# One attention step split in two, the mLSTM gates moved ahead of the convolution, and a new order of the first loads in a two-layer hybrid trunk

## The chip, the cores and the metric

The kernel runs on one core of one Trainium2 chip. The metric is the device time of one execution in microseconds (us). Before the change three runs gave 2652.69, 2652.71 and 2653.03 us, median 2652.71 us.

## What is computed

A trunk of two layers on 1024 tokens of width 1024. Each layer projects the normalised input once and gives its columns to three groups of heads, called mixers here; then come an output projection, an MLP and a gated extra input, each added to x:

```python
h = rms_norm(x);  y = h @ w_in + b_in
m_out = mlstm(...)      # 4 heads x 64: causal conv + SiLU on q and k, gates, chunkwise state
h_out = hgrn2(...)      # 4 heads, state 64 x 64, chunkwise gated recurrence
s_out = swa(...)        # 8 query heads, 2 kv heads x 64, window 128, one sink per head
x = x + concat(m_out, h_out, s_out) @ w_out
x = x + square(relu(rms_norm(x) @ w_up)) @ w_down
x = x + sigmoid(rms_norm(x) @ w_g) * rms_norm(p[l] @ w_p)
```

In the attention the probabilities are `exp(s - m) / (sum exp(s - m) + exp(sink - m))`. In the mLSTM the gates are cumulative sums and running maxima over time of the two pre-activations `mi` and `mf`; the convolution works on q and k alone, so neither needs the other before the scores are weighted.

## The kernel before, in words

The tokens are cut in two halves b = 0, 1 of 512, and every dense product works on one half. A dense product (`gemm`, lines 409 to 441) keeps fp32 accuracy with three products per weight tile: each operand is split in a high part (`whi`, ACT, line 395) and a low rest (`wlo`, DVE, line 399), and high x high, high x low and low x high are added up in PSUM. One step of `gemm` is one pair of weight tiles: 24 matmuls of 128x512 on TensorE (lines 435 and 437). There are four `whi` and four `wlo` buffers, two steps' worth.

The mixers are Python generators: `SWA` (attention), `HGRN` and `MLSTM`, one for each 256 tokens of a half. Each `yield` ends one mixer step. The `Emitter` runs the dense work as the main program and, after each dense step, adds `rate` to a counter and emits one mixer step for every whole one; up to three mixers take turns. The rate is 1.9 and 2.5 in the two input projections of the first layer (`IN(0,0)` and `IN(0,1)`), 0.7 in those of the second, and `RATE_MLP` = 0.9 in the MLP, whose 66 dense steps of a half carry the mixers of the other half. Before a half's output projection `OUT_T` (line 685) transposes the mixers' results. The emission order is a priority; the order in which each engine's instructions finally stand is fixed when the program is built, and each engine works through its own in that order. So an instruction that waits holds up all that stands behind it on its engine.

The places that the change and the prediction touch:

- `SWA`, lines 887 to 1005: one step makes the scores of a block of 128 queries (L969) and the exponentials (L979). The next step divides each of eight heads by its sum (L989, DVE), transposes the probabilities (L999, TensorE) and copies them out (L1001, ACT). In the step after that `values` (L932) multiplies them with V: for each half of the window two matmuls, one per kv head, that write different halves of the columns.
- `MLSTM`, lines 1178 to 1302: step one is the convolution (ACT L1192, twelve DVE operations L1194); step two the two SiLUs of q and k, the copies into `qbd`, and then the gates: transposes L1209 on TensorE, a log-sigmoid on ACT (L1215, L354 to L356), two scans and some small operations on DVE (L1217 to L1231) into `G`. Step three transposes `G` (L1236). Later steps use the SiLU results (L1262), make the products with the state (L1272, L1277, L1283) and end with `head_out`, whose last instruction is L1035.
- `load_x`, lines 520 to 532, makes the first loads: x of the first half on the queues of SP and ACT (L527), and between them the first two tiles of weights `w_skv` (`early`). ACT then issues the `cols` constants (L184), the positions, and one row of biases (L555).
- `first`, lines 1341 to 1350, interleaves the first normalisation `a` with the first projection `c`. The normalisation ends with the root of the mean square (L483 to L349) and its transposes (L574).

In MLP and PLE, L498 transposes the normalised x, L794 transposes p.

Of the kernel before, what the change touches and what calls it, by code (L numbers as in the profile page):

```python
# [16 lines left out]
AF = mybir.ActivationFunctionType  # L17
ALU = mybir.AluOpType
# [20 lines left out]
RATE_IN00 = 1.9  # L39
RATE_IN01 = 2.5  # L40
RATE_IN = 0.7
RATE_MLP = 0.9
RATE_PLE = 0.9

ROOM = tuple(22 - 4 * max(0, (n + 2) // 4) + 2 for n in range(24)) + (8,)
# [4 lines left out]
C_IN, C_MLP, C_PLE, C_CW, C_CB, C_BF, C_MG, C_LB = 0, 8, 16, 24, 40, 44, 52, 56  # L50
# [106 lines left out]
class Trunk:  # L157
# [362 lines left out]
    def load_x(self, b, src, first=False):  # L520
        X = [[None, None] for _ in range(4)]
        for h in range(2):
            for t in range(4):
                s = X[t][h] = self.get()
                eng = self.nc.gpsimd if not first else self.nc.scalar if (h, t % 2) == (0, 1) else self.nc.sync
                with self.tc.high_priority(2000) if first and h == 0 else nullcontext():
                    end = eng.dma_start(s[:, :512], src(b, t, h))  # L527
                    if first and h == 0 and t == 3:
                        self.x_asked = end
            if first and h == 0:  # L530
                self.early = [self.wraw(self.skv_rows(0, kp)) for kp in range(2)]
        return X

    def x_in(self, b, t, h):
# [352 lines left out]
    def SWA(self, l, b, hb, st):  # L887
        nc, rs = self.nc, self.rs[l]
# [48 lines left out]
        for i in range(2):  # L937
# [25 lines left out]
            for hp in range(4):  # L963
# [8 lines left out]
                for j in range(2):  # L972
                    h = 2 * hp + j
# [3 lines left out]
                for j in range(2):  # L977
                    h = 2 * hp + j
# [8 lines left out]
            for h in range(8):  # L987
                v = PX[h // 2][:, (h % 2) * n:(h % 2) * n + n]
                nc.vector.tensor_scalar(v, v, rsum[:, h:h + 1], None, op0=ALU.mult)  # L989

            vis = (prev, cur)[2 - n // P:]
            pts = [[None, None] for _ in vis]
            for kv in range(2):
                for hf in range(len(vis)):
                    ps = self.bank()
                    for g in range(4):
                        h = kv * 4 + g
                        c = (h % 2) * n + hf * P
# [179 lines left out]
    def MLSTM(self, l, b, hb, st):  # L1178
        nc, cols, ident = self.nc, self.cols[l], self.ident
# [3 lines left out]
        if b == 0 and hb == 0:  # L1183
            nc.gpsimd.memset(self.cbd, 0.0)
            nc.gpsimd.memset(self.ml, 0.0)
        Y = [self.get() for _ in range(2)]
        a = self.get()
        for f in range(4):
            y = Y[f // 2][:, (f % 2) * 256:(f % 2) * 256 + 256]
            u = st["U"][f]  # L1190
            c0 = C_CW + 4 * f
            nc.scalar.activation(y, u[:, hb * 256:hb * 256 + 256], AF.Identity, scale=cols[:, c0:c0 + 1], bias=cols[:, C_CB + f:C_CB + f + 1])  # L1192
            for j in range(1, 4):
                nc.vector.scalar_tensor_tensor(y, u[:, hb * 256 + j:hb * 256 + j + 256], cols[:, c0 + j:c0 + j + 1], y, op0=ALU.mult, op1=ALU.add)  # L1194
        if hb == 1:
            self.put(*st["U"])
        yield
        Q, Kt = Y[0][:, :512], Y[1][:, :512]
        self.silu(Q, a[:, :512])
        self.silu(Kt, a[:, :512], 0.125)  # L1200
        Q3 = Q.rearrange("p (a t) -> p a t", a=2)
        K3 = Kt.rearrange("p (a t) -> p a t", a=2)
        for j in range(2):
            nc.vector.tensor_copy(self.qbd[j * 64:j * 64 + 64, :, j, :], Q3[j * 64:j * 64 + 64])

        pg = self.bank()
        for i in range(2):
# [22 lines left out]
        nc.vector.tensor_copy(Gb[32:36], r1)  # L1230
        nc.vector.tensor_tensor(Gb[64:68], r1, Gb[32:36], op=ALU.subtract)  # L1231
        self.put(g, g2)
        yield
        pt = self.bank()
        for c in range(2):
# [14 lines left out]
        for c in range(2):  # L1250
# [33 lines left out]
            for h in range(4):  # L1284
                r, p = (h % 2) * 64, h // 2
# [13 lines left out]
        self.head_out(H[:, :512], mo[:, :512], a[:, :512], ms, False)  # L1299
        self.put(H, ND, kw, a, *Y, mv)  # L1300
        self.release_kv(st["skv"][hb])
# [3 lines left out]
def chain(*gens):  # L1305
    for g in gens:
        yield from g


@with_exitstack  # L1310
def trunk_kernel(ctx: ExitStack, tc: tile.TileContext, io, dims):
    k = Trunk(ctx, tc, io, dims)
    L = k.L
    assert k.NB == 2
    st = {}
    for l in range(L):
        st[l, 0], st[l, 1] = {}, {}
    em = Emitter(k.S_, WIDTH)
    last = L - 1

    def IN(l, b, between=None):
        return k.IN(l, b, st[l, b], lambda kind: em.queue.extend(k.MIX(l, b, st[l, b], kind)), between)

    def norm(l, b):
        return k.IN_norm(l, b, st[l, b])

    def OUT(l, b):
        if "own" not in st[l, b]:
            em.flush((l, b), 0)
            k.OUT_T(l, b, st[l, b])  # L1330
        em.run(k.OUT(l, b, st[l, b]))

    def tail(l, b, then=None):
        def ready():
            em.flush(then)
            k.OUT_T(*then, st[then])

        em.run(k.MLP(l, b), RATE_MLP)
        em.run(k.PLE(l, b, l == last, ready if then else None), RATE_PLE)

    def first():
        a, c = norm(0, 0), IN(0, 0, norm(0, 1))
        yield next(a)
        yield next(c)
        k.behind = k.last_mm
        yield next(c)
        yield next(a)
        k.behind = None
        yield from a
        yield from c  # L1350

    em.run(first(), RATE_IN00)
    k.bounds()
    em.run(IN(0, 1), RATE_IN01, ROOM, (0, 0))
    OUT(0, 0)
    for l in range(L):
        tail(l, 0, (l, 1))
        OUT(l, 1)
        if l == last:
            tail(l, 1)  # L1360
            break
        em.run(chain(norm(l + 1, 0), IN(l + 1, 0)), RATE_IN)
        tail(l, 1, (l + 1, 0))
        OUT(l + 1, 0)
        em.run(chain(norm(l + 1, 1), IN(l + 1, 1)), RATE_IN)
# [51 lines left out]
```

## Time and profile before

| | |
|---|---|
| median of three runs | 2652.71 us |
| the profiled execution | 2653.13 us |
| its span in the trace | 2651.4 us |
| TensorE busy | 2636.1 us (99%) |
| DVE busy | 1742.0 us (66%) |
| ACT busy | 1401.5 us (53%) |
| granted TensorE clock, mean | 0.999 |

The span is the time from the first to the last instruction in the trace; the execution itself took 1.7 us more. Times in the rows are microseconds from the start of the span. A matmul's end is modelled: matmuls overlap, so the durations of one engine's rows may add up to more than the time between their starts, and a wait is read best from start to start. L12 is line 12 of the kernel before.

### The profile page before, as it was taken

Reading aid. Unit: us, or ns where it says so; the run is one execution under the profiler, and the core shown is the slowest. Engines: PE = TensorE matmul, PEld = TensorE weight load, DVE = VectorE, ACT = ScalarE, POOL = GpSimd, SP = SyncE. Lnnn points to the kernel's source line nnn. Section 1 sums busy time; section 2 is a strip of 40 time slices with the busy share of each in tenths; the row PEclk is TensorE's granted clock in tenths of the full one; section 3 lists DMA queues with packets and bytes.
Section 4 is the critical chain, followed back from the end, with each engine's and each line's share of the span. In section 5 each row is a group of like instructions: output and inputs, shape, how many; then the busy total and the mean of one; then the engine's idle time right before and its main releaser. Section 6 shows DMA issues by size and latency. Waiting matters only on the chain.

```text
span 2651.4 us, 35073 instructions
## 1 busy us (share of the span) xinstructions
PE 2636.1 (99%) x12719; PEld 2143.3 (81%) x12719; DVE 1742.0 (66%) x3697; ACT 1401.5 (53%) x2924; POOL 106.1 (4%) x232
## 2 busy tenths in 40 slices
PE   9999999999999999999999999999999999999999
PEld 7877788887788888887788888888778888888887
DVE  5787757677678557776775755776677584443448
ACT  5456545455557544545654653554664464433336
POOL 3201100000000100000000010000000000000000
PEclk9999999999999999999999999999999999999999
DMA  7644532222222532222222253222222243332332
GB/s 220 199 115 121 144 110 80 88 80 80 84 84 90 151 100 80 88 87 73 80 88 96 97 155 93 77 88 80 78 82 88 96 135 104 96 96 95 104 104 80
DMA packets 138845, 270.54 MB, mean 102 GB/s; under 512 B 10672, under 2 KB 15920, under 8 KB 138672
## 3 DMA queue, kind: packets, MB, share of 16 engines
q1 hardware_dynamic: 119328, 224.03, 27.2%
q0 software_dynamic: 18480, 43.55, 5.5%
q8 instruction: 100, 1.64, 0.3%
q10 hardware_dynamic: 864, 0.72, 0.1%
q14 instruction: 73, 0.60, 0.1%
HBM read 249.39 MB, written 18.87 MB: 101 GB/s over the span
## 4 chain that ended last, share of the span: by engine, by line
PE 95%; DVE 2%; ACT 1%; issue 1%; DMA 1%; POOL 0%; POOLq 0%; ACTq 0%; DVEq 0%
PE gbank L437 52%; PE gbank L435 32%; PE mbank L498 1%; PE mbank L932 1%; PE mbank L999 1%; PE mbank L1142 1%; PE mbank L969 1%; PE gbank L467 1%; PE mbank L1262 1%; PE mbank L1269 1%; PE mbank L1158 0%; PE mbank L1127 0%; PE mbank L945 0%; PE mbank L1272 0%; ACT junk L476 0%
## 5 line engine op out<-in xcount | busy, mean ns | idle before, releaser
L437 PE MATMUL gbank<-whi,slot 128*128 128x512 f32 (+1 forms) x4160 | 1303.2, 391 | 0.0
L395 ACT ACTIVATE whi<-raw 128x512 fp32r<-128x512 f32 (+1 forms) x836 | 515.2, 621 | 830.7 <-PE gbank L437 492.1
L437 PEld LDWEIGHTS gbank<-whi,slot 128*128 128x128 f32 x4160 | 772.1, 188 | 170.4 <-issue 2.8
L399 DVE TENSOR_TENSOR wlo<-raw,whi 128x512 fp32r<-128x512 f32 (+1 forms) x800 | 538.3, 679 | 545.2 <-ACT whi L395 542.2
L435 PE MATMUL gbank<-slot,whi 128*128 128x512 f32 x2560 | 824.7, 397 | 0.0
L437 PE MATMUL gbank<-wlo,slot 128*128 128x512 f32 (+1 forms) x2080 | 807.9, 389 | 0.4 <-DVE wlo L399 0.3
L435 PEld LDWEIGHTS gbank<-slot,whi 128*128 128x128 f32 x2560 | 480.3, 188 | 110.7 <-issue 3.3
L435 PE MATMUL gbank<-slot,wlo 128*128 128x512 f32 x1280 | 505.9, 395 | 0.5 <-DMA wlo<-lo 0.4
L437 PEld LDWEIGHTS gbank<-wlo,slot 128*128 128x128 f32 x2080 | 391.5, 188 | 81.2 <-DVE wlo L399 0.8
L435 PEld LDWEIGHTS gbank<-slot,wlo 128*128 128x128 f32 x1280 | 241.1, 188 | 52.3 <-DMA wlo<-lo 1.3
L759 DVE SCALAR_TENSOR_TENSOR slot<-gbank,nrs,slot 128x512 f32<-128x512 f32 x256 | 191.4, 748 | 48.7 <-PE gbank L437 45.6
L367 DVE TENSOR_TENSOR slot<-slot 128x512 fp32r<-128x512 f32 x144 | 99.1, 690 | 86.9 <-ACT slot L366 86.1
L370 DVE SCALAR_TENSOR_TENSOR slot<-mbank,cols,slot 128x512 fp32r<-128x512 f32 x112 | 78.8, 744 | 20.3 <-ACT slot L369 20.0
L745 ACT ACTIVATE slot<-gbank 128x512 f32<-128x512 f32 x128 | 74.9, 585 | 32.4 <-PE gbank L435 32.3
L366 ACT ACTIVATE slot<-slot 128x512 fp32r<-128x512 f32 x144 | 89.6, 629 | 2.6
L369 ACT ACTIVATE slot<-mbank,cols 128x512 fp32r<-128x512 f32 x112 | 72.3, 686 | 20.7 <-PE mbank L498 14.8
L746 ACT ACTIVATE slot<-slot 128x512 f32<-128x512 f32 x128 | 80.6, 629 | 2.5
L476 ACT ACTIVATE junk<-slot 128x512 bf16<-128x512 f32 x96 | 60.1, 626 | 34.3 <-DVE slot L759 16.9
L979 ACT ACTIVATE slot<-slot,snm 128x256 f32<-128x256 f32 (+1 forms) x128 | 61.8, 484 | 29.2 <-DVE snm L976 29.2
L788 POOL DMA_DIRECT2D slot<-in_p_dram x8 | 5.7, 719 | 1412.1 <-PE gbank L437 469.8
L498 PE MATMUL mbank<-ident,slot 128*128 128x128 f32 x384 | 60.7, 273 | 0.5 <-ACT slot L1259 0.5
L1096 ACT ACTIVATE slot<-slot 128x256 f32<-128x256 f32 x56 | 23.5, 420 | 71.3 <-DVE slot L1095 71.1
(274 smaller groups left out, 2287.3 us busy)
## 6 DMA issues: line engine op xcount, KB each, us to landing
raw<-in_w_up_dram SPq DMA_DIRECT2D x128, 512.0 KB, 3.6
raw<-in_w_down_dram SPq DMA_DIRECT2D x128, 512.0 KB, 3.5
raw<-in_w_in_dram SPq DMA_DIRECT2D x80, 512.0 KB, 3.8
raw<-in_w_ple_gate_dram SPq DMA_DIRECT2D x32, 512.0 KB, 3.5
lo<-wlo POOLq DMA_DIRECT2D x40, 256.0 KB, 4.3
wlo<-lo POOLq DMA_DIRECT2D x40, 256.0 KB, 3.0
raw<-in_w_out_dram SPq DMA_DIRECT2D x16, 512.0 KB, 4.4
raw<-in_w_out_dram SPq DMA_DIRECT2D x32, 256.0 KB, 4.3
```

The lines of the kernel that those rows point to most:

```text
L366: first = nc.scalar.activation(r_(hi), src, AF.Copy)
L367: nc.vector.tensor_tensor(r_(lo), src, hi, op=ALU.subtract)
L369: first = nc.scalar.activation(r_(hi), src, AF.Copy, scale=scale)
L370: nc.vector.scalar_tensor_tensor(r_(lo), src, scale, hi, op0=ALU.mult, op1=ALU.subtract)
L395: nc.scalar.activation(hi[:, :n], raw[:, kk, :n], AF.Copy)
L399: nc.vector.tensor_tensor(lo[:, :n], raw[:, kk, :n], hi.bitcast(F32)[:, :n], op=ALU.subtract)
L435: nc.tensor.matmul(banks[i], wa[:, sl], ta, start=first, stop=last)
L437: self.last_mm = nc.tensor.matmul(banks[i][:, :n], ta, wa[:, :n], start=first, stop=last)
L498: nc.tensor.transpose(ps[:, t * P:(t + 1) * P], X[t][h][:, k4 * P:(k4 + 1) * P], self.ident)
L745: nc.scalar.activation(u[:, :512], ps, AF.Relu)
L746: nc.scalar.activation(u[:, :512], u[:, :512], AF.Square)
L759: nc.vector.scalar_tensor_tensor(x, ps, r2[:, i:i + 1], x, op0=ALU.mult, op1=ALU.add)
```

## The change

Four pieces. The numerical work is the same, instruction for instruction; only the order changes.

- In `SWA` a `yield` is put between the division of the probabilities and their transposes, so these are two mixer steps.
- In `MLSTM` the gates come first, as a step of their own; then the convolution, as before a step; then the SiLUs ("scale"), now a step of their own.
- `RATE_MLP` goes from 0.9 to 1.0. For one half the three kinds of mixers had 64 steps to run, counting the last resumption of each; now there are 70, because each attention mixer has two more and each mLSTM one more.
- The first two `w_skv` loads are to stand behind the second x load of SP, and `first` emits one more step of the projection before the normalisation's end.

```diff
-RATE_MLP = 0.9
+RATE_MLP = 1.0
...
                     if first and h == 0 and t == 3:
                         self.x_asked = end
+                    if first and h == 0 and t == 2:
+                        self.x_sp = end
             if first and h == 0:
-                self.early = [self.wraw(self.skv_rows(0, kp)) for kp in range(2)]
+                with self.tc.issue_after(self.x_sp.ins):
+                    self.early = [self.wraw(self.skv_rows(0, kp)) for kp in range(2)]
...
             for h in range(8):
                 v = PX[h // 2][:, (h % 2) * n:(h % 2) * n + n]
                 nc.vector.tensor_scalar(v, v, rsum[:, h:h + 1], None, op0=ALU.mult)
+            yield
...
     def MLSTM(self, l, b, hb, st):
...
-        Y = [self.get() for _ in range(2)]
-        a = self.get()
-        for f in range(4):
...
-        yield
-        Q, Kt = Y[0][:, :512], Y[1][:, :512]
-        self.silu(Q, a[:, :512])
-        self.silu(Kt, a[:, :512], 0.125)
...
-            nc.vector.tensor_copy(self.qbd[j * 64:j * 64 + 64, :, j, :], Q3[j * 64:j * 64 + 64])
         pg = self.bank()
...
         nc.vector.tensor_tensor(Gb[64:68], r1, Gb[32:36], op=ALU.subtract)
         self.put(g, g2)
+        yield
+        Y = [self.get() for _ in range(2)]
+        a = self.get()
+        for f in range(4):
...
+        yield
+        Q, Kt = Y[0][:, :512], Y[1][:, :512]
+        self.silu(Q, a[:, :512])
+        self.silu(Kt, a[:, :512], 0.125)
...
+            nc.vector.tensor_copy(self.qbd[j * 64:j * 64 + 64, :, j, :], Q3[j * 64:j * 64 + 64])
         yield
         pt = self.bank()
...
     def first():
         a, c = norm(0, 0), IN(0, 0, norm(0, 1))
         yield next(a)
         yield next(c)
         k.behind = k.last_mm
         yield next(c)
         yield next(a)
         k.behind = None
+        yield next(c)
         yield from a
         yield from c
```

How the order of the built program moves is shown at three places. The first is SP's queue at the start of the program; L527 are loads of x, L377 loads of weights. Before:

```order
L527 DMA slot<-in_x_dram 128x512
L377 DMA raw<-in_w_skv_dram 128x2x264
L527 DMA slot<-in_x_dram 128x512
L377 DMA raw<-in_w_skv_dram 128x2x264
L527 DMA slot<-in_x_dram 128x512 x4
L377 DMA raw<-in_w_skv_dram 128x2x264 x2
```

Now:

```order
L527 DMA slot<-in_x_dram 128x512 x2
L377 DMA raw<-in_w_skv_dram 128x2x264 x2
L527 DMA slot<-in_x_dram 128x512 x4
L377 DMA raw<-in_w_skv_dram 128x2x264 x2
L377 DMA raw<-in_w_in_dram 128x2x512 x20
```

SP's second x load has moved ahead of the first weight load; nothing else moved in this queue.

The second place is DVE's queue in `IN(0,1)`, at the first mLSTM: L989 is the last attention division before it, L1194 the convolution, L357 of 128x512 and L1019 belong to the SiLU of q, L357 of 4x256 to L1224 are the gates. Before:

```order
L989 TENSOR_SCALAR slot<-slot,srs 128x256 x8
L1194 SCALAR_TENSOR_TENSOR slot<-slot,cols_93 128x256 x12
L357 SCALAR_TENSOR_TENSOR slot<-slot 128x512
L1019 TENSOR_TENSOR slot<-slot 128x512
L357 SCALAR_TENSOR_TENSOR slot<-slot 4x256
L1204 COPY qbd<-slot 64x2x256 x2
L1217 SCALAR_TENSOR_TENSOR slot<-rmask,slot 4x256
L1218 SCALAR_TENSOR_TENSOR slot<-slot,ml,mbank 4x256
L1221 TENSOR_TENSOR G_345<-mbank,slot 4x256
L357 SCALAR_TENSOR_TENSOR slot<-slot 128x512
L1220 TENSOR_TENSOR G_345<-slot 4x256
L1224 TENSOR_SCALAR G_345<-slot 4x256
```

Now (L992 is the old L989, L1202 to L1216 the old L1217 to L1231, L1227 the old L1194):

```order
L992 TENSOR_SCALAR slot<-slot,srs 128x256 x8
L357 SCALAR_TENSOR_TENSOR slot<-slot 4x256
L1202 SCALAR_TENSOR_TENSOR slot<-rmask,slot 4x256
L1203 SCALAR_TENSOR_TENSOR slot<-slot,ml,mbank 4x256
L1206 TENSOR_TENSOR G_379<-mbank,slot 4x256
L1205 TENSOR_TENSOR G_379<-slot 4x256
L1209 TENSOR_SCALAR G_379<-slot 4x256
L1207 TENSOR_SCALAR G_379<-G_379,ml 4x128
L1208 TENSOR_SCALAR G_379<-G_379,slot 4x128
L1210 COPY ml<-slot 4x1
L1213 CAST Gb<-G_379 4x256
L1227 SCALAR_TENSOR_TENSOR slot<-slot,cols_93 128x256
```

The gates stand alone and ahead of the convolution. On TensorE the distance between the transposes that open the gates (old L1209) and those that close them (old L1236) changes with it: in `IN(0,1)` from 45 and 68 dense matmuls to 19 and 26, in the MLPs from 24 to 51 or 52. In `IN(0,1)` the last products of the mLSTM (old L1283) stand 91 dense matmuls ahead of `OUT_T` (old L685) before the change, and 45 now.

The third place is TensorE in the MLP of the first layer's first half, at the last products of attention with V. Before (L932 are those products, L435 and L437 dense matmuls):

```order
L437 MATMUL gbank<-whi,slot 128x512
L932 MATMUL mbank<-slot,V 64x512
L437 MATMUL gbank<-whi,slot 128x512
L437 MATMUL gbank<-wlo,slot 128x512
L437 MATMUL gbank<-whi,slot 128x512 x2
L437 MATMUL gbank<-wlo,slot 128x512
L437 MATMUL gbank<-whi,slot 128x512
L932 MATMUL mbank<-slot,V 64x512 x2
L437 MATMUL gbank<-whi,slot 128x512
```

Now (L935 is the old L932):

```order
L435 MATMUL gbank<-slot,wlo 128x512
L435 MATMUL gbank<-slot,whi 128x512
L935 MATMUL mbank<-slot,V 64x512 x4
L435 MATMUL gbank<-slot,whi 128x512
L435 MATMUL gbank<-slot,wlo 128x512
L435 MATMUL gbank<-slot,whi 128x512 x2
```

The four products, which were cut 1, 2, 1 by six dense matmuls each, stand together now.

## Rows read from the trace of the kernel before

**Rows 1.** The page, engines: busy time, share of the span, instructions.

```profile
PE 2636.1 (99%) x12719; PEld 2143.3 (81%) x12719; DVE 1742.0 (66%) x3697; ACT 1401.5 (53%) x2924; POOL 106.1 (4%) x232
```

**Rows 2.** The page, the chain that ended last: shares of the span by engine.

```profile
PE 95%; DVE 2%; ACT 1%; issue 1%; DMA 1%; POOL 0%; POOLq 0%; ACTq 0%; DVEq 0%
```

**Rows 3.** The chain in order of time, at 562: start, duration, what.

```profile
562.04 22.21 PE gbank L435 x96
```

**Rows 4.** Timeline, start: start, duration, engine, line [idle before, releaser].

```profile
6.99 1.91 PE L498 MATMUL mbank<-ident,slot 128*128 128x128 f32 x16
7.29 0.40 ACTq L555 DMA_DIRECT2D slot<-in_rowB_dram  x1
7.80 0.69 ACT L369 ACTIVATE slot<-mbank,cols 128x512 fp32r<-128x512 f32 x1 [5.71 <-DMA cols<-in_cols_dram]
...
23.52 0.62 PE L574 MATMUL mbank<-ident,nrs 128*128 128x128 f32 x4 [0.41 <-DVE nrs L349]
```

**Rows 5.** Timeline, TensorE: the two transposes of the gates in IN(0,1).

```profile
267.88 0.41 PE L1236 MATMUL mbank<-ident,G 100*128 100x100 f32 x2 [0.91 <-DVE G L1222]
...
299.50 0.28 PE L1236 MATMUL mbank<-ident,G 100*128 100x100 f32 x1 [1.00 <-DVE G L1222]
```

**Rows 6.** Timeline, ACT and DVE: the gates' chain before the first of them.

```profile
258.57 0.45 ACT L1215 ACTIVATE slot<-mbank,fb 4x256 f32<-4x256 f32 x1
...
262.99 0.41 DVE L357 SCALAR_TENSOR_TENSOR slot<-slot 4x256 f32<-4x256 f32 x1
...
264.20 0.68 DVE L1217 TENSOR_TENSOR_SCAN slot<-rmask,slot 4x256 f32<-4x256 bf16 x1
...
267.45 0.28 DVE L1222 TENSOR_SCALAR G<-G,ml 4x128 f32<-4x128 f32 x1
```

**Rows 7.** Timeline, TensorE and DVE: end of the mixers in IN(0,1).

```profile
313.56 0.61 PE L1283 MATMUL mbank<-slot 128*128 128x130 f32 x4
...
323.48 0.69 DVE L1035 TENSOR_TENSOR slot<-slot 128x512 f32<-128x512 f32 x1 [0.62 <-ACT slot L361]
...
335.14 1.91 PE L685 MATMUL mbank<-ident,slot 128*128 128x128 f32 x16
```

**Rows 8.** Timeline, TensorE: end of the first MLP and its PLE.

```profile
793.96 0.41 PE L1236 MATMUL mbank<-ident,G 100*128 100x100 f32 x2 [0.84 <-DVE G L1222]
...
803.18 0.66 PE L498 MATMUL mbank<-ident,slot 128*128 128x128 f32 x4 [0.55 <-ACT slot L1259]
```

**Rows 9.** Timeline, TensorE: from L1277 to L1283 in one mLSTM chunk.

```profile
274.94 0.38 PE L1277 MATMUL mbank<-ident,slot 128*128 128x128 f32 x2
...
276.08 0.61 PE L1283 MATMUL mbank<-slot 128*128 128x130 f32 x4
```

**Rows 10.** Timeline, TensorE: attention transposes in the MLP of (0,1).

```profile
1201.94 0.40 PE L435 MATMUL gbank<-slot,whi 128*128 128x512 f32 x1
...
1203.58 1.50 PE L999 MATMUL mbank<-ident,slot 128*128 128x128 f32 x7 [0.41 <-DVE slot L989]
1204.84 0.48 PE L437 MATMUL gbank<-whi,slot 128*128 128x512 f32 x1
```

**Rows 11.** Timeline, TensorE: first piece of the V products cut in three.

```profile
700.16 1.07 PE L932 MATMUL mbank<-slot,V 128*64 128x512 f32 x2
701.16 0.50 PE L437 MATMUL gbank<-whi,slot 128*128 128x512 f32 x1
```

**Rows 12.** Timeline, TensorE: V products in one piece.

```profile
634.21 1.94 PE L932 MATMUL mbank<-slot,V 128*64 128x512 f32 x8
636.08 0.50 PE L435 MATMUL gbank<-slot,whi 128*128 128x512 f32 x1
```

**Rows 13.** Busy time in stretches: us, PE, PEld, DVE, ACT, POOL (x instructions), clock, DMA.

```profile
255.01:270.20 15.19, 14.28 (x68) 10.89 (x65) 13.22 (x32) 9.93 (x21) 2.12 (x4) 1.00 0.41 123
...
720.00:760.00 40.00, 39.94 (x202) 32.57 (x201) 22.89 (x47) 18.95 (x40) 1.44 (x2) 1.00 0.30 94
2319.00:2363.00 44.00, 44.00 (x192) 35.77 (x191) 19.09 (x28) 16.47 (x29) 0.00 (x0) 1.00 0.30 96
```

More of the change, by code (lines that the diff above doesn't have):

```diff
@@ L1185, in MLSTM @@
             nc.gpsimd.memset(self.ml, 0.0)
-        Y = [self.get() for _ in range(2)]
-        a = self.get()
-        for f in range(4):
[L1189 to L1196, printed above, removed]
-        yield
-        Q, Kt = Y[0][:, :512], Y[1][:, :512]
-        self.silu(Q, a[:, :512])
-        self.silu(Kt, a[:, :512], 0.125)
-        Q3 = Q.rearrange("p (a t) -> p a t", a=2)
-        K3 = Kt.rearrange("p (a t) -> p a t", a=2)
-        for j in range(2):
-            nc.vector.tensor_copy(self.qbd[j * 64:j * 64 + 64, :, j, :], Q3[j * 64:j * 64 + 64])
         pg = self.bank()
@@ L1232, in MLSTM @@
         self.put(g, g2)
+        yield
+        Y = [self.get() for _ in range(2)]
+        a = self.get()
+        for f in range(4):
+            y = Y[f // 2][:, (f % 2) * 256:(f % 2) * 256 + 256]
+            u = st["U"][f]
+            c0 = C_CW + 4 * f
+            nc.scalar.activation(y, u[:, hb * 256:hb * 256 + 256], AF.Identity, scale=cols[:, c0:c0 + 1], bias=cols[:, C_CB + f:C_CB + f + 1])
+            for j in range(1, 4):
+                nc.vector.scalar_tensor_tensor(y, u[:, hb * 256 + j:hb * 256 + j + 256], cols[:, c0 + j:c0 + j + 1], y, op0=ALU.mult, op1=ALU.add)
+        if hb == 1:
+            self.put(*st["U"])
+        yield
+        Q, Kt = Y[0][:, :512], Y[1][:, :512]
+        self.silu(Q, a[:, :512])
+        self.silu(Kt, a[:, :512], 0.125)
+        Q3 = Q.rearrange("p (a t) -> p a t", a=2)
+        K3 = Kt.rearrange("p (a t) -> p a t", a=2)
+        for j in range(2):
+            nc.vector.tensor_copy(self.qbd[j * 64:j * 64 + 64, :, j, :], Q3[j * 64:j * 64 + 64])
         yield
```

## Prediction, made before the changed kernel was run

> **What bounds the kernel now.** I read the page first. TensorE is busy for 2636.1 of 2651.4 us, 99% [rows 1], and 95% of the chain that ended last is TensorE's own work [rows 2]. A busy TensorE need not be a fast one, so the next view is the chain in order of time: there 96 dense matmuls take 22.21 us [rows 3], 0.231 us each, and the clock column beside such stretches reads 1.00, the 2.4 GHz level [rows 13]. The change removes no matmul. What it can win is the time in which TensorE does nothing, and all of that is 2651.4 - 2636.1 = 15.3 us. Part of it, the wait for the first data and the output after the last matmul, no order removes. So I went through TensorE's timeline and looked for waits over 0.25 us. There are few, and each has a name: at the start [rows 4], at the transposes of the gates [rows 5, 8], at attention's transposes [rows 10] and at products that are cut up [rows 11]. The reader is to see in these rows that the sum is one of single microseconds; 0.2%, or 5.3 us, is about what a measurement of this kernel can tell from no change.
>
> At one point a rule speaks otherwise. By rows, headroom is 15.3 us. The Trainium skill (Perfetto Trace Analysis, Identifying the Most-Contended Engine) holds that the busy share of matmuls says little and that the busy share of weight loads should be used for TensorE; that share is 81% here. By it an estimated 500 us would be open, and a better order could win far more than the list below. The pitch of 0.231 us, which is the same wherever a long run of dense matmuls stands, is why I sum by rows.
>
> **Part 1, the start.** The second x load of SP now goes ahead of a weight load. Before, TensorE's first transposes start at 6.99, and ACT's first use of them at 7.80, after ACT has issued the bias row at 7.29 [rows 4]. In the built program that issue waits for the landing of the second weight load before, and for the smaller constants now. At most the 7.80 becomes 6.99 + 4 x 0.11 (four transposes, 16 in 1.91 us less overlap), a gain of 0.4, if x does not come earlier too; at least nothing. I take 0.3. The next step of the projection is emitted ahead of the normalisation's end, so two more matmuls stand before the transposes L574, which wait for 0.41 us now [rows 4]; the ACT work ahead of them is the same. I take 0.4 of the two kinds of wait there. Together -0.7, between 0 and -1.8 (all the waits of 8 to 24 us and the 0.4).
>
> Here too a rule is weighed. Rows show x, weights and constants all issued in the first 8 us and ACT waiting 5.71 us for the last of what it needs [rows 4]. The Trainium skill (DMA: Bandwidth & Descriptors, Issuing engines are not separate DMA queues) says that all queues end in the same 16 engines and interleave, so moving one load ahead only delays another. By it this term would be 0 instead of -0.7, which the bounds contain.
>
> **Part 2, the first layer's input projections.** Up to the first third of `IN(0,1)` TensorE's order is the same, so its waits there stay. Then come the gates. Before, TensorE idles 0.91 and 1.00 us at L1236 for `G` [rows 5]. The chain to `G` is: ACT L1215 at 258.57, then three operations of 4x256; DVE's log-sigmoid, scans and differences until 267.45 + 0.28 [rows 6], 9.2 us, because the SiLUs and the copies lie between. Alone it is about 1.7 us on ACT (four like L1215's 0.45, or a little less), 0.5 for L357, and 3.5 from L1217 to the end of L1222 less the 0.6 of a SiLU between: some 5.2 us. The first transposes now come 19 dense matmuls, 4.4 us, behind the gates' start: a wait of 0.8. At the second, 26 matmuls, 6.0 us: a wait of 0.2 for what DVE still has. So -0.1 and -0.8, -0.9. What is late next is `head_out`: six more steps at the same rate end the mixers later. From L1283 at 313.56 to the end of L1035 at 323.48 + 0.69 it takes 10.6 us [rows 7]; before, 91 matmuls (21 us) cover that, and L685 comes at 335.14. Now 45 do, 10.4 us, and DVE has the evacuations of the last dense product in between. I add 0.5, between 0 and 2.5 (two such evacuations and one weight split more). Together -0.4, between -1.9 and +2.
>
> **Part 3, the MLPs.** In the MLPs the gates' transposes now have 51 matmuls of cover, 11.8 us against 5.2: the 0.84 of [rows 8] goes, with 0.17 more, since a dense matmul's row lasts 0.40 [rows 10] and its pitch 0.231: -1.0. But at that place the built order now puts L1283 straight behind L1277, and from the one to the other take 1.14 us [rows 9], 0.22 of them two transposes: +0.9. The 0.55 behind it [rows 8] I take as overlapped by this one, -0.4. Together -0.5, between -1.7 and +0.9.
>
> The division step: with a step between, L999 finds its operand ready. In the MLP of (0,1) TensorE goes from 1201.94 to 1204.84 through eight transposes [rows 10]; one pitch of 0.231 and 8 x 0.11 would be 1.11: -1.8. The products with V run two at a time when they stand together: eight in 1.87 us [rows 12]. Cut in three, each piece takes 1.00 us [rows 11], and there are three pieces: 3.0 - 1.87 and two changes between kinds of matmul less, -1.3. Smaller waits of this kind in MLPs I leave out. Together -3.1; at least half of it, -1.5, and at most -3.6.
>
> The rate: 70 steps over 66 dense steps instead of 64 at 0.9 need the same stretch. DVE carries them: 19.09 us per eight dense steps without mixers [rows 13], 2.4 per step of 5.55, and 13.22 for a whole convolution, SiLU and gates [rows 13], now over three steps instead of two. I cost this at nothing, since TensorE has been busy for 39.94 of 40 us in a stretch that has the heavier two-step form [rows 13].
>
> **Part 4, what the new order may cost.** The built order also puts steps of HGRN closer behind the transposes at the start of two MLPs, and cuts some transposes of attention in two. Nothing in the trace of before shows them. Below, 0; above, a wait of 1.0 and one of 0.5 (the sizes of [rows 5, 8]) at each of two places, 3.0. I take +0.7, nearer to nothing, because most of the waits over 0.25 lie in `IN(0,1)`.
>
> **Sum.** -0.7 - 0.4 - 0.5 - 3.1 + 0.7 = -4.0 us. The profiled execution took 2653.13 us, 1.7 more than its span and 0.4 more than the median of 2652.71; from the median it comes to **2648.7 us**.
>
> **The rivals.** *All waits go and none comes.* -1.8 - 1.9 - 1.7 - 3.6 = -9.0; with two thirds of it, 2646.7, with all 2643.7. For it: the waits have names and the change aims at each. Against: in `IN(0,1)` the new cover is shorter, not longer. Chance 0.25.
>
> *The waits move.* `head_out`, L1283 and the start of the MLPs take what the gates and the start gave: -0.7 + 2 + 0.9 + 2 - 3.1 - 1.0 (the one of rows 8) = +0.1, with half of these costs 2650.5, with all 2652.8. For it: 45 matmuls against a chain of 10.6 us. Chance 0.22.
>
> *It does not do what it says.* The final order is not the emission order. If the attention transposes end up waiting as before, only parts 1 and 2 remain, 2651.6. Against: the order shown has the V products together. Chance 0.06.
>
> *DVE becomes the bound, and it is slower.* The three mLSTM steps now fall on three dense steps in a row: 13.2 + 3 x 2.4 = 20.4 us of DVE against 3 x 5.55 + 0.8 = 17.5 of TensorE, 2.9 too much. If the weight splits on DVE are queued behind that, TensorE waits for `wlo`. Six such passes lie in MLPs: +17.4, with -4.0 it gives 2666.1. It decides from the point where the buffers of split weights hold less than 2.9 us of work; they hold one step ahead, 5.55. Against it: before, the two-step form is 13.2 + 2.2 x 2.4 = 18.5 against 2.2 x 5.55 = 12.2, 6 us too much, and TensorE idled 0.06 us there [rows 13]. Chance 0.03.
>
> *The rule on weight loads is right, and much is open.* By rows as a mechanism: if the 0.231 us contained a stall that order removes, the stretches with mixers would have a longer pitch than [rows 3]; they do not. A hundredth of the span, 26 us less, would be 2626. Chance 0.02.
>
> **How the numbers follow.** The forecast itself has 0.42 and reaches from 2646.5 to 2650.5. Faster by over 0.2% (below 2647.4) holds the rule, two thirds of the first rival and a quarter of the forecast: 0.02 + 0.17 + 0.11 = 0.30. Slower by over 0.2% (above 2658.0) is DVE's case and a hundredth for the rest: 0.04. Within 0.2%: 0.66. The range of 8 in 10 leaves out the far ends of the first rival and of the second: 2645.5 to 2652.3.
>
> **What would show it.** Right: in the changed trace no idle time before L999 and L1236 in the MLPs, V products in one piece of about 1.9 us; idle before L1236 of 0.8 and 0.2 in `IN(0,1)`; L685 within a microsecond of the 1152nd dense matmul; ACT's first use of the transposes by 7.5. Wrong: TensorE idle before L435 or L437 for `wlo`, more than 2.5 us before L685, or a start later than before.

## The result, and the profile after

The changed kernel takes 2668.56 us (median of three runs, 2667.18 to 2670.51) against 2652.71 before: 15.85 us slower, ratio 1.0061, 95% interval 1.0043 to 1.0079. The forecast was 2648.7 with a range up to 2652.3, and slower by over 0.2% had 0.04. The range did not hold the time.

The page of the changed kernel, engines and then the chain that ended last, which answer to [rows 1, 2]:

```profile
PE 2639.6 (99%) x12719; PEld 2143.7 (80%) x12719; DVE 1736.9 (65%) x3697; ACT 1396.5 (52%) x2924; POOL 106.4 (4%) x232
...
PE 93%; DVE 5%; ACT 1%; issue 1%; DMA 0%; ACTq 0%; DVEq 0%
```

The span is 2666.8 us, so TensorE is idle for 27.2 us where it was 15.3, and busy for 3.5 us more with the same number of instructions. Both have to be explained: 11.9 us of waits, and 3.5 us in which the same matmuls took longer. VectorE (DVE) has no more to do than before (1736.9 against 1742.0), but its share of the chain went from 2% to 5%. The waits view of TensorE says who is waited for (line waited at, releaser: us in total, times, longest):

```profile
PE gbank L437 <- DVE wlo L399: 9.6, 6, 3.1
PE mbank L1241 <- DVE G L1207: 2.1, 2, 1.2
PE gbank L435 <- DVE slot L762: 1.6, 5, 0.6
...
PE gbank L435 <- DVE wlo L399: 1.3, 2, 0.7
```

Before, `wlo` cost L437 0.3 us in one wait. Now the low halves of the weights (L399) and the evacuations of the down projection (L762) come late. Where? The table gives, for the dense matmul that has the given number of dense matmuls ahead of it, its start in each trace minus its start in the trace of before. A stage's cost is the difference of two rows. The runs e1 to e13 are those of the next section. In the middle of a stage the numbers mean little, because mixers may run earlier or later there; these are ends of stages.

| dense matmul, place | after | e1 | e2 | e3 | e7 | e8 | e9 | e13 |
|---|---|---|---|---|---|---|---|---|
| 1152, end of `IN(0,1)` | 0.3 | 1.2 | 1.1 | -0.9 | 0.3 | -0.3 | 2.8 | 1.5 |
| 3888, start of the MLP (0,1) | 0.0 | 5.2 | 1.7 | -3.5 | -2.4 | -4.0 | 3.7 | 6.3 |
| 5424, its end | 7.2 | 7.6 | 5.3 | -3.3 | -1.8 | -5.9 | 5.0 | 9.0 |
| 6432, start of the MLP (1,0) | 7.7 | 8.7 | 5.9 | -3.2 | -1.3 | -5.6 | 5.3 | 9.4 |
| 7968, its end | 15.0 | 9.8 | 10.0 | -2.3 | 0.4 | -6.3 | 7.9 | 12.0 |
| last | 15.4 | 11.0 | 10.7 | -1.6 | 0.9 | -5.4 | 8.5 | 12.3 |

Nearly all of the net loss is made in two MLPs, 7.2 and 7.3 us. Here is the worst place in the first of them, TensorE's timeline (start, duration, engine, line; in brackets the idle time before it and who ended it):

```profile
1326.81 0.50 PE L437 MATMUL gbank<-whi,slot 128*128 128x512 f32 x1
1327.15 0.34 PE L1260 MATMUL mbank<-Gb,selb 128*128 128x128 bf16 x3
1330.57 0.79 PE L437 MATMUL gbank<-wlo,slot 128*128 128x512 f32 x1 [3.08 <-DVE wlo L399]
...
1332.02 0.63 PE L437 MATMUL gbank<-wlo,slot 128*128 128x512 f32 x1
1332.44 0.63 PE L437 MATMUL gbank<-whi,slot 128*128 128x512 f32 x1
...
1338.14 0.39 PE L437 MATMUL gbank<-wlo,slot 128*128 128x512 f32 x1
```

TensorE waits for nothing but `wlo` here, and stands for 3.08 us. Behind the wait the pitch of dense matmuls, from start to start, is 0.43 us instead of 0.23. And this is what ACT and DVE did meanwhile, in the timeline of all engines:

```profile
1319.72 1.13 ACT L395 ACTIVATE whi<-raw 128x512 fp32r<-128x512 f32 x2
...
1320.68 0.67 DVE L399 TENSOR_TENSOR wlo<-raw,whi 128x512 fp32r<-128x512 f32 x1
1321.38 0.42 DVE L1214 TENSOR_TENSOR slot<-G,Gb 4x256 f32<-4x256 f32 x1
1321.83 0.48 DVE L1227 SCALAR_TENSOR_TENSOR slot<-slot,cols 128x256 f32<-128x256 f32 x1
1322.35 0.28 DVE L1215 CAST Gb<-slot 4x256 bf16<-4x256 f32 x1
1322.66 1.41 DVE L762 SCALAR_TENSOR_TENSOR slot<-gbank,nrs,slot 128x512 f32<-128x512 f32 x2
1324.11 0.42 DVE L1216 TENSOR_TENSOR Gb<-slot,Gb 4x256 bf16<-4x256 f32 x1
1324.55 0.75 DVE L762 SCALAR_TENSOR_TENSOR slot<-gbank,nrs,slot 128x512 f32<-128x512 f32 x1
...
1325.22 0.87 DVE L1227 SCALAR_TENSOR_TENSOR slot<-slot,cols 128x256 f32<-128x256 f32 x2
1326.01 0.74 DVE L762 SCALAR_TENSOR_TENSOR slot<-gbank,nrs,slot 128x512 f32<-128x512 f32 x1
1326.67 3.24 DVE L1227 SCALAR_TENSOR_TENSOR slot<-slot,cols 128x256 f32<-128x256 f32 x8
...
1329.84 0.68 DVE L399 TENSOR_TENSOR wlo<-raw,whi 128x512 fp32r<-128x512 f32 x1
```

Both `whi` tiles of the step were ready by 1319.72 + 1.13 = 1320.85. Its first `wlo`, for which TensorE waits, came at 1329.84; counted tile by tile, the L399 at 1320.68 is the last of the step before. For 9.0 us the instruction stood in VectorE's queue behind the end of that L399, the end of the gates (L1214 to L1216, 1.1 us), four evacuations (2.9) and eleven of the twelve convolution operations (L1227, 4.6); these three are 8.6 us. The Trainium skill (DVE: scalar operands, raw-bit mode, write accounting and state across instructions; Flops that outlive an instruction) calls the queue of this engine "one in-order queue"; these rows agree.

### The profile page after: what moved, and what is told of

Same layout as the page of the kernel before. It is cut to its first block, busy times and chain, and to the rows that moved or that the text cites. A ratio compares the mean times of both kernels' runs of the same rounds, so it can differ in the third digit from the quotient of the medians.

```text
span 2666.8 us, 35061 instructions
## 1 busy us (share of the span) xinstructions
PE 2639.6 (99%) x12719; PEld 2143.7 (80%) x12719; DVE 1736.9 (65%) x3697; ACT 1396.5 (52%) x2924; POOL 106.4 (4%) x232
## 3 DMA queue, kind: packets, MB, share of 16 engines
q1 hardware_dynamic: 119328, 224.03, 27.2%
## 4 chain that ended last, share of the span: by engine, by line
PE 93%; DVE 5%; ACT 1%; issue 1%; DMA 0%; ACTq 0%; DVEq 0%
PE gbank L437 50%; PE gbank L435 32%; PE mbank L498 1%; PE mbank L935 1%; PE mbank L972 1%; PE mbank L1003 1%; PE mbank L1146 1%; DVE slot L1227 1%; PE gbank L467 1%; DVE slot L762 1%; PE mbank L1267 1%; PE mbank L1274 0%; PE mbank L1162 0%; DVE wlo L399 0%; DVE slot L1153 0%
## 5 line engine op out<-in xcount | busy, mean ns | idle before, releaser
L437 PE MATMUL gbank<-whi,slot 128*128 128x512 f32 (+1 forms) x4160 | 1303.4, 391 | 0.2
L437 PEld LDWEIGHTS gbank<-whi,slot 128*128 128x128 f32 x4160 | 773.0, 188 | 171.9 <-issue 2.0
L399 DVE TENSOR_TENSOR wlo<-raw,whi 128x512 fp32r<-128x512 f32 (+1 forms) x800 | 538.5, 679 | 570.8 <-ACT whi L395 567.8
L435 PE MATMUL gbank<-slot,whi 128*128 128x512 f32 x2560 | 829.0, 397 | 1.9 <-DVE slot L762 1.6
L437 PE MATMUL gbank<-wlo,slot 128*128 128x512 f32 (+1 forms) x2080 | 809.7, 390 | 9.7 <-DVE wlo L399 9.6
L435 PEld LDWEIGHTS gbank<-slot,whi 128*128 128x128 f32 x2560 | 479.7, 188 | 114.6 <-DVE slot L762 4.3
L435 PE MATMUL gbank<-slot,wlo 128*128 128x512 f32 x1280 | 505.1, 395 | 1.4 <-DVE wlo L399 1.3
L437 PEld LDWEIGHTS gbank<-wlo,slot 128*128 128x128 f32 x2080 | 392.0, 189 | 94.2 <-DVE wlo L399 11.8
L435 PEld LDWEIGHTS gbank<-slot,wlo 128*128 128x128 f32 x1280 | 240.8, 188 | 52.5 <-DVE wlo L399 2.1
L762 DVE SCALAR_TENSOR_TENSOR slot<-gbank,nrs,slot 128x512 f32<-128x512 f32 x256 | 190.8, 747 | 39.0 <-PE gbank L437 36.8
L367 DVE TENSOR_TENSOR slot<-slot 128x512 fp32r<-128x512 f32 x144 | 99.1, 689 | 95.7 <-ACT slot L366 95.5
L366 ACT ACTIVATE slot<-slot 128x512 fp32r<-128x512 f32 x144 | 89.6, 628 | 2.9
```

What stands on the lines that cost most here:

```text
L366: first = nc.scalar.activation(r_(hi), src, AF.Copy)
L367: nc.vector.tensor_tensor(r_(lo), src, hi, op=ALU.subtract)
L399: nc.vector.tensor_tensor(lo[:, :n], raw[:, kk, :n], hi.bitcast(F32)[:, :n], op=ALU.subtract)
L435: nc.tensor.matmul(banks[i], wa[:, sl], ta, start=first, stop=last)
L437: self.last_mm = nc.tensor.matmul(banks[i][:, :n], ta, wa[:, :n], start=first, stop=last)
L762: nc.vector.scalar_tensor_tensor(x, ps, r2[:, i:i + 1], x, op0=ALU.mult, op1=ALU.add)
```

## The experiments

Each ratio is against runs of the kernel before on the same chip. The lead of e4 and e7 is the number of places by which the builder draws the loads and splits of the weights forward in its order (AHEAD). A pass is one run of an mLSTM mixer over 256 tokens.

| run | what | us | ratio, 95% interval |
|---|---|---|---|
| e1 | rate back at 0.9 | 2664.84 | 1.0044 (1.0030 to 1.0058) |
| e2 | division step back | 2664.12 | 1.0043 (1.0030 to 1.0055) |
| e3 | mLSTM's steps back | 2651.11 | 0.9992 (0.9984 to 1.0001) |
| e4 | lead of the weight splits 80 | 2657.44 | 1.0016 (1.0007 to 1.0025) |
| e5 | gates and convolution in one step | 2674.85 | 1.0080 (1.0066 to 1.0094) |
| e6 | convolution, SiLU, gates | 2649.88 | 0.9989 (0.9980 to 0.9998) |
| e7 | lead 80 in the MLPs alone | 2654.89 | 1.0008 (1.0000 to 1.0017) |
| e8 | convolution, gates, SiLU | 2647.64 | 0.9980 (0.9971 to 0.9989) |
| e9 | the change, one step later | 2662.21 | 1.0037 (1.0024 to 1.0050) |
| e10 | e8, one step later | 2648.64 | 0.9986 (0.9977 to 0.9994) |
| e11 | a third of the convolution | 2653.08 | 1.0002 (0.9993 to 1.0011) |
| e12 | e8 without the division step | 2656.45 | 1.0014 (1.0005 to 1.0023) |
| e13 | mLSTM's new order alone | 2664.94 | 1.0047 (1.0034 to 1.0059) |
| e14 | rate 1.0 alone | 2655.78 | 1.0011 (1.0002 to 1.0020) |
| e15 | division step and start alone | 2659.18 | 1.0025 (1.0016 to 1.0035) |

**Which part of the change is it?** Three theories: A, only rate, division step and order together make the steps meet badly; B, the gates-first order does it; C, the rate does it.

```diff
e1  -RATE_MLP = 1.0
    +RATE_MLP = 0.9
e2  -            yield      (SWA, between division and transposes)
e3   MLSTM: the two steps of the kernel before, in their old order
```

> The changed kernel with the rate in the MLPs back at 0.9 mixer steps per dense step; the rest of the change stays. Theory A (a meeting in VectorE's queue: gates, convolution and the evacuations of a down projection fall on the same dense steps only where rate, division step and the gates-first order come together): the waits of 3.2 us at L437 for wlo go, 2648 to 2655 us. Theory B (the gates-first order by itself makes VectorE too dense for three dense steps): most of the loss stays, 2660 us or more. Theory C (a rate of 1.0 by itself makes VectorE the bound): the loss goes, 2648 to 2655 us, as by A.

> The changed kernel without the new step between attention's division and its transposes; rate 1.0 and the gates-first order stay. Theory A: mLSTM's steps come some dense steps earlier and no longer meet the evacuations; the waits of 3.2 us go, while the waits at attention's transposes (2 to 4 us in all) come back: 2650 to 2657 us. Theory B: the order is still there, 2662 us or more. Theory C: the rate is still there, 2662 us or more.

> The changed kernel with mLSTM's steps in their old form and order (convolution; SiLU and gates in one step); rate 1.0, division step and start stay. Theory A: the meeting is gone, 2648 to 2656 us. Theory B: gone as well, 2648 to 2656 us. Theory C: the rate alone carries the loss, 2662 us or more, and with the heavier two-step form over 2 dense steps rather more than less.

e1 keeps 11.8 us of the loss, e2 11.1; e3 loses nothing, with the full rate. C is out, A as it was put is out, B stands. But rate and division step have a share in the price: by the table the two MLPs lose 14.5 us in the change, 3.5 in e1 and 7.7 in e2. Not all of e1's loss is `wlo`: 5.2 us arise before the MLP (0,1). TensorE's waits view of e1 names a line of the PLE, L810, beside L399:

```profile
PE gbank L437 <- DVE wlo L399: 3.4, 5, 1.1
PE gbank L437 <- DVE slot L810: 2.8, 2, 2.6
```

By the program, at 0.9 the 66 dense steps of an MLP carry 59 of 70 mixer steps; the rest falls into the next stage.

**What in the new order?** B1: the convolution behind the gates; B2: the third step.

```diff
e5   gates + convolution | SiLU
e6   convolution | SiLU | gates
e8   convolution | gates | SiLU
```

> The changed kernel with gates and convolution in one mixer step, SiLU in the next: the new order, but two steps as before. Theory B1 (what hurts is that the convolution stands right behind the gates, whose chain holds VectorE back for 5 us first): the waits for wlo stay or grow, 2662 us or more. Theory B2 (what hurts is the third step, which spreads the same work over one dense step more and lets it run into the next evacuations): they go, 2649 to 2655 us.

> The changed kernel with mLSTM's three steps in the old order: convolution, SiLU, gates. Theory B1: the convolution does not stand behind the gates, the waits for wlo go, those of the gates' transposes for G stay at 0.6 to 0.9 us a piece: 2649 to 2655 us. Theory B2: three steps as in the changed kernel, most of the loss stays, 2660 us or more.

> The changed kernel with mLSTM's three steps as convolution, gates, SiLU: the convolution ahead of the gates, and one step between the gates and their transposes as the change wanted. Theory B1: no waits for wlo, and those for G shrink as well: 2648 to 2651 us, the best so far. Theory B2: most of the loss stays, 2660 us or more.

All three speak for B1, though e8 came out 0.4 us below its range. e5 is the slowest of all. e6 and e8, with three steps, the same instructions, rate and division step as the changed kernel, have no wait for `wlo` at all, and e8 is the fastest kernel of this study: 0.9980 of before, 20.9 us under the change. The difference is visible long before the place that stalls. The timeline of e8, all engines, first pass in the MLP (0,1):

```profile
1291.03 2.09 ACT L1197 ACTIVATE slot<-slot,cols 128x256 f32<-128x256 f32 x4
1291.69 4.57 DVE L1199 SCALAR_TENSOR_TENSOR slot<-slot,cols 128x256 f32<-128x256 f32 x11 [1.88 <-ACT slot L1197]
...
1314.31 0.60 PE L1206 MATMUL mbank<-ident,slot 128*4 128x128 f32 x4
```

The convolution needs nothing of TensorE in this stage, so where it stands first it runs when VectorE has time (1.88 us idle before it), 23.3 us and some four dense steps before TensorE reaches the gates' transposes. In the timeline of the kernel before it is the same:

```profile
1299.25 2.07 ACT L1192 ACTIVATE slot<-slot,cols 128x256 f32<-128x256 f32 x4
...
1325.66 0.60 PE L1209 MATMUL mbank<-ident,slot 128*4 128x128 f32 x4
```

In the changed kernel the gates' operations stand ahead of it, and they wait for the transposes, which TensorE makes when it gets there (timeline of the change):

```profile
1312.70 0.60 PE L1194 MATMUL mbank<-ident,slot 128*4 128x128 f32 x4
...
1313.39 0.45 ACT L1200 ACTIVATE slot<-mbank,fb 4x256 f32<-4x256 f32 x1
...
1317.75 1.08 ACT L1225 ACTIVATE slot<-slot,cols 128x256 f32<-128x256 f32 x2
```

So the convolution starts 5.1 us after the transposes instead of 23 to 26 us before them, and gates and convolution reach VectorE as one lump.

**Is it the place in the queue, or the load?**

```diff
e4  -AHEAD = 40
    +AHEAD = 80
e7   the same 80, in em.run(k.MLP(...)) alone
e11 -            for j in range(1, 4):
    +            for j in range(1, 2):
```

> The changed kernel with a lead of 80 instructions instead of 40 for the weight splits in the builder's order; no work is added or taken away, L399 only stands further ahead in VectorE's queue. Theory A in its queue form (L399 is late because convolution instructions stand ahead of it, VectorE has time enough over the MLP as a whole): the waits for wlo go, 2648 to 2655 us. If VectorE's sheer load in these steps is the cause (B, C), something else on VectorE becomes late in its place, the evacuations L762 or the gates: 2660 us or more.

> The changed kernel with the lead of the weight splits at 80 instructions in the MLPs alone, 40 elsewhere. If the loss is a matter of who stands ahead of whom in VectorE's queue, the two MLPs lose 0.4 and 2.0 us as with a lead of 80 everywhere, and the 3.5 us that the start lost there do not come: 2651 to 2656 us. If VectorE's load in these steps is the cause whatever the order, the waits only move to evacuations or gates: 2660 us or more.

> The changed kernel with one of the three VectorE taps of the convolution (L1227) instead of three: 8 of 12 operations of 0.40 us are left out per pass, so the convolution computed is another one. If VectorE's backlog behind the gates is what holds wlo back, 3.2 us less of it per pass takes away the waits of 3.2 us and the clock's fall behind them: 2646 to 2652 us. If the order of the steps matters in another way (TensorE's own order, ScalarE), most of the loss stays: 2660 us or more.

e7 adds and removes no work; it lets L399 stand further ahead (and the load and the `whi` of the same tile, which TensorE did not wait for in the change). 13.7 of the 15.85 us go, and what is left of the waits for `wlo` in TensorE's waits view (L400 and L438 there, one line further down) is

```profile
PE gbank L438 <- DVE wlo L400: 1.8, 2, 0.9
```

So the place in the queue decides. e4 lies in neither of its ranges (2657.44): it is 2.6 us slower than e7, and it loses this at the start, where the longer lead applies too. Its 300th dense matmul comes 3.2 us later than before, that of e7 at the same time. e11 leaves work out instead, and it helps as much (2653.08), but not all the way to the 2647.64 of e8: it lies 1 us above its own range, 2646 to 2652, and 2.6 us of waits for `wlo` stay. Where the convolution stands weighs more than two thirds of its work.

**Is it the phase?** R: the lump hurts wherever it falls. P: only where it meets the evacuations.

```diff
e9   the change, with a "yield" ahead of mLSTM's first operation
e10  e8, with the same "yield"
```

> The changed kernel with one empty mixer step ahead of each mLSTM pass: same steps in the same order, one dense step later in the MLP. Theory R (run-ahead: behind the gates the convolution can't run before TensorE has reached the gates' transposes, so gates and convolution are one lump of 10 us on VectorE wherever it falls): waits for wlo stay in the MLPs, 2658 us or more. Theory P (phase: the lump hurts only where it meets the four evacuations L762 of a down projection): the second layer's waits of 3.2 us go, 2648 to 2655 us.

> The order convolution, gates, SiLU (the fastest so far, 2647.6 us) with one empty mixer step ahead of each mLSTM pass. Theory R: the convolution runs some three dense steps ahead of TensorE in any phase, no waits for wlo come: 2646 to 2650 us. Theory P: one dense step later means other neighbours, waits for wlo of 1 to 3 us in several passes: 2653 us or more.

Both times lie in the ranges of R, and the waits speak for it: e10 has none for `wlo`, e9 has seven. But P has a large share. The longest wait of e9 is 1.1 us instead of 3.1, and by the table its two MLPs lose 1.3 and 2.6 us instead of 7.2 and 7.3; that e9 is over 2658 owes much to the 3.7 us that arise before them. The order makes the waits, the phase sets most of their price. The waits view of e9, TensorE:

```profile
PE gbank L437 <- DVE wlo L399: 3.2, 4, 1.1
...
PE gbank L435 <- DVE wlo L399: 1.9, 3, 0.7
```

**The parts alone.** What was open: whether the order costs without the rest, and what rate and division step are worth by themselves.

```diff
e12  e8 without the "yield" in SWA
e13  before, with MLSTM as changed
e14  before, with RATE_MLP = 1.0
e15  before, with the "yield" in SWA and the changed start
```

> The order convolution, gates, SiLU without the new step between attention's division and its transposes. The difference to 2647.6 us is what that step is worth where VectorE is not late: by the sum of the prediction 3.1 us, so 2650 to 2652 us. If the waits before L1003 and the cut products were covered by something else, nothing: 2647 to 2649 us.

> The kernel before with mLSTM's three steps in the new order (gates, convolution, SiLU) and nothing else of the change; rate 0.9. Theory R (the order by itself ties the convolution behind the gates): waits for wlo in the MLPs though neither the rate nor attention has changed, 2656 us or more. If it takes the rate of 1.0 or the division step as well: 2650 to 2654 us.

> The kernel before with a rate of 1.0 in the MLPs and nothing else. Theory C (a rate of 1.0 makes VectorE the bound) is out by the runs with the old order; what is left is the phase of every mixer step in the MLP: 2651 to 2656 us, with no wait for wlo over 1.5 us.

> The kernel before with the new step between attention's division and its transposes and with the changed start; mLSTM's order and the rate of 0.9 as before. If the step is worth the 8.8 us that it was worth beside the order convolution, gates, SiLU at a rate of 1.0: 2644 to 2646 us. If at 0.9 the longer list of steps runs past the end of the MLP and gives it back: 2649 to 2656 us.

e13 settles the first: mLSTM's part of the change alone (new order and third step), at the old rate and with the old attention, brings waits for `wlo`, 5.2 us in TensorE's waits view, and costs 11.9 us:

```profile
PE gbank L437 <- DVE wlo L399: 2.8, 5, 1.0
PE gbank L435 <- DVE wlo L399: 2.4, 3, 1.0
```

By the table 5.3 of the 11.9 us arise in the two MLPs; 6.3 arise before them, most of it in the stage behind the MLP (0,0), where TensorE waits for the splits of the normalised x (1.3 us for L366, 1.4 for L367). What the third step costs at a rate of 0.9 was not run by itself; at 1.0, with the convolution first, it costs nothing (e6, e8).

The rate alone costs 2.75 us, within its expectation, and with one wait of 0.4 us for `wlo` it is not that mechanism. The division step was missed on both sides. Undone beside e8 it was worth 8.8 us, not 3.1; alone, at 0.9, it loses 6.2 us. There the longer list runs past the MLP, and two transposes of the gates in the stage behind it wait 4.06 us (TensorE's timeline):

```profile
819.10 0.57 PE L1240 MATMUL mbank<-ident,G 100*128 100x100 f32 x2 [4.06 <-DVE G L1228]
```

Part of the 8.8 may be phase, since every later step moves with the step that is taken out; this is not shown. How much is the step's own, these runs don't separate.

## Why the prediction was wrong

**The step that failed** is "The rate" in part 3, the only place where the sum weighs what mLSTM's three new steps do to VectorE. It said of VectorE's load, now over three steps: "I cost this at nothing, since TensorE has been busy for 39.94 of 40 us in a stretch that has the heavier two-step form [rows 13]". That stretch, 720 to 760, has no convolution in it. In DVE's timeline of before, the last convolution operations of one pass and the first of the next are

```profile
700.21 1.01 DVE L1194 SCALAR_TENSOR_TENSOR slot<-slot,cols 128x256 f32<-128x256 f32 x2
...
764.65 0.48 DVE L1194 SCALAR_TENSOR_TENSOR slot<-slot,cols 128x256 f32<-128x256 f32 x1
```

I took the step in which an instruction is emitted for the time at which it runs. The two-step form was never heavy where I looked, since its first step had run some four dense steps earlier. It was that distance that hid the convolution, and the change took it away. So waits for `wlo` and L762, with what followed from them, cost 19.7 us where the sum had nothing. The load by itself does no harm: e6 and e8 carry the same three steps at the same rate. The error is in the reordering, which I had priced only where it shortens TensorE's wait for the gates, not in the rate (e3, e13).

**The rival that came nearest** had 0.03: DVE becomes the bound, TensorE waits for `wlo`, six passes at 2.9 us, 2666.1. It named the wait, and the six passes are all there. Summed over waits and slow matmuls behind them, those for `wlo` and L762 cost, in the first and the second pass, 1.9 and 1.9 us in the MLP (0,0), 6.7 and 1.8 in (0,1), 5.5 and 1.9 in (1,0): 19.7 us, 3.3 a pass. I dismissed it with the same two-step form: "6 us too much, and TensorE idled 0.06 us there". Its reason, too much load in three dense steps, is not what the runs show (e6, e8), and the passes are far from alike, so its time is right in part by luck. The lead of the split weights, which it put at 5.55 us, was 6.3 at the worst place (ready at 1320.85, wanted behind the matmul at 1326.81). It weighed 2.9 us of excess load against that; what counted was the 8.6 us of work queued ahead of L399.

**The other terms** come to 15.4 - 19.7 = -4.3 us, where the whole forecast was -4.0. That these agree is luck in part: up to the end of `IN(0,1)` the table has +0.3 where the sum had -1.1.

- *Start, -0.7:* the first dense matmul comes 0.39 us earlier, the 300th 0.18. No gain is shown by this: in e8, with the same start, the 300th comes 0.81 later than in before, and in e14, with the old start, 0.47 later. The traces of single executions differ by as much as the term. The 0 that was weighed beside -0.7 fits no worse, and no run tests the start by itself.
- *`IN(0,1)`, -0.4:* from the 300th to the 1152nd matmul +0.4. The idle times before the gates' transposes were to be 0.8 and 0.2 (before, [rows 5]); TensorE's timeline has

```profile
262.82 0.28 PE L1241 MATMUL mbank<-ident,G 100*128 100x100 f32 x1 [0.89 <-DVE G L1207]
...
296.49 0.28 PE L1241 MATMUL mbank<-ident,G 100*128 100x100 f32 x1 [1.25 <-DVE G L1207]
```

  The first chain took 5.4 us from the transposes, as worked out (5.2). The second took 7.4, since parts of `head_out` stood between its operations on DVE. The wait that I put before L685 did not come; in e9 it did (0.66 us).

- *MLPs, -0.5 and -3.1:* L1241 waits in no MLP now (before, 0.84 in [rows 8]), and eight transposes L1003 take 1.02 us from matmul to matmul where [rows 10] took 2.9. The V products that were cut in three [rows 11] run in one piece. L1288 waits, as was forecast (+0.9); it comes 0.80 us late, start to start. TensorE's timeline:

```profile
691.26 1.94 PE L935 MATMUL mbank<-slot,V 128*64 128x512 f32 x8
...
804.07 0.71 PE L1288 MATMUL mbank<-slot 128*128 128x130 f32 x4 [0.63 <-DVE slot L1284]
...
1191.66 0.39 PE L435 MATMUL gbank<-slot,whi 128*128 128x512 f32 x1
1191.89 1.04 PE L1003 MATMUL mbank<-ident,slot 128*128 128x128 f32 x8
1192.68 0.48 PE L435 MATMUL gbank<-slot,whi 128*128 128x512 f32 x1
```
- *New order, +0.7:* L1160 waits twice, 0.35 us each start to start.

"TensorE idle before L435 or L437 for `wlo`" was named as what would make the forecast wrong, and it did.

**The weight loads.** The Trainium skill (Perfetto Trace Analysis, Identifying the Most-Contended Engine) would read TensorE's headroom from the busy share of weight loads. It stayed at 80 to 81% from the fastest kernel here to the slowest, over 27 us of difference; the waits view told them apart.

## What to carry to other kernels

Before pricing a moved step, look up in the trace when its instructions ran, not when they were emitted: work that needs nothing of the busiest engine may be running far ahead of it, and that lead is lost when it is put behind work that waits for that engine. Put the independent work first (here convolution, gates, SiLU, 2647.64 us), and give the instruction that feeds the bound engine a place ahead of both. A stretch that is to show that a load is harmless must be seen to contain the load.

## What the runs showed of the hardware that was not expected

A wait of 3.1 us cost TensorE more than 3.1 us, because the granted clock fell in it and stayed low behind it. Stretches of the changed kernel (us, PE, PEld, DVE, ACT, POOL, clock, DMA share, GB/s):

```profile
1320.00:1326.00 6.00, 5.36 (x24) 4.00 (x23) 5.80 (x14) 2.01 (x4) 0.00 (x0) 1.00 0.28 87
...
1332.00:1334.00 2.00, 2.00 (x6) 1.59 (x5) 2.00 (x6) 0.68 (x2) 0.00 (x0) 0.50 0.67 168
...
1338.00:1340.00 2.00, 2.00 (x11) 1.62 (x10) 1.80 (x3) 2.00 (x7) 0.00 (x0) 1.00 0.00 0
```

The clock is 0.50 (1.2 GHz) from 1329.5, 1.1 us before the wait ends, up to 1336.3, and 13 dense matmuls take 5.71 us, where 13 at 0.231 take 3.0: 2.7 us on top. Behind the second such wait (3.09 us, in the MLP (1,0)) it was 2.9 us at the low clock and 1.4 us on top. Of the 15.4 us, 4.1 are this, more than the 3.5 us net by which TensorE is busy longer. Behind the waits of up to 1.1 us in e9 the clock stays at 1.00:

```profile
1335.00:1340.00 5.00, 4.03 (x25) 3.20 (x24) 5.00 (x11) 2.53 (x4) 0.00 (x0) 1.00 0.16 37
```

It stays there behind the 2.6 us for L810 in e1 too. In e13 it falls to 0.50 at 807.1 us, when TensorE had waited for L366 (1.3 us, until 802.85) and for L367 (1.4 us, until 806.87). So the length of one wait does not tell whether the clock falls.

The Trainium skill (TensorE: Matmul & The Clock Gate, Wait — 56ns, not 53.3ns?) gives start to start of 426.7 ns at 512 columns and 1.2 GHz, and 215.7 at 2.4 GHz. The first agrees with the 0.427 measured here; at the upper level these matmuls take 0.231, and the measured number was used.
